# Pairwise sums of the weight blocks: moving those of the down projection from the second attention into the first gate-and-up stage

## The chip, the cores and the metric

One Trainium2 chip; the kernel uses one of its cores. The metric is device time in microseconds (us) of one launch. Lower is better.

## The reference, cut to what matters

One layer (DEPTH = 1): a chunked attention with a relative-position bias, then a SwiGLU feed-forward network (FFN), each between two RMS norms. 2048 tokens, width 1024, 16 heads of 64, d_ff 2816, all in float32.

```python
h = rms_norm(x, g_pre_mix)
m = chunk_relpos_attention(h, w_qkv, w_o, rel_bias)   # chunk c of 64 sees chunks c-8..c
x = x + rms_norm(m, g_post_mix)
h = rms_norm(x, g_pre_ffn)
x = x + rms_norm((silu(h @ w_gate) * (h @ w_up)) @ w_down, g_post_ffn)
```

## The kernel before, in words

**Precision.** Each float32 operand is split into a rounded part `hi` and a rest `lo`; a product is three TensorE (PE) matmuls (`products`, lines 189 to 191). The text calls these three a *triple*.

**Stages.** The tokens form two groups of 1024 (`NG` = 2), each with two halves of 512. In order of time: attention of group 0, attention of group 1 (their query, key, value and output products interleaved with scores, softmax and values), then for each group `gate_up(g, ...)` and `down(g, ...)`. The attentions are driven by a loop over 64 slots per group at the end of the code; in each slot `Attend.scores` and `Attend.transposed` run with dense products as fill.

**Seven products instead of eight.** Gate, up and down are 2x2 block products done with seven block multiplications (a Strassen-Winograd scheme). Four of the seven need weight blocks that are sums of given blocks, called S1 to S4. These sums do not depend on the tokens. They are made once, in DRAM, by DMAs alone: `copy` writes one block to its place (SP's queue), and `add` adds another to it with an accumulating DMA (POOL's queue, line 857). A *unit* is one slice of the weights: 11 units for gate and up (blocks of 512 KB, tensors `gu_S`), 11 for down (256 KB, `d_S`), with four copies and four adds each. `weight_sums` is a generator of *steps*; the copies of unit u stand in steps 4u to 4u+3, its adds in steps 4u+5, 4u+6, 4u+8 and 4u+11. The copies are put on SP's queue behind the last DMA issued there, the adds on POOL's behind the last softmax scaling (`pool.tensor_scalar`, line 566).

**When the steps are issued before.** 22 units give 96 steps; slot m of the 128 slots of both attentions issues the next step whenever `m * 96 // 120` grows: 0.8 step per slot. Gate and up come first, so nearly all of their sums fall in the first attention, and those of down in the second.

**Order.** The order of PE is written out by hand. On each other engine the instructions run in one fixed order too. Side work (norms, late residual sums, loads for later) waits in the queue `later`; each triple of PE earns one unit of credit (`tick`), and a step of `later` runs when its cost is there.

**The first gate-and-up stage.** `gate_up(0, ...)` runs 11 rounds of seven products, each of 8 triples. Each product takes one 512 KB weight block, loaded up to four products ahead (`ffn_ahead`), split on ACT and DVE. Beside it, `later` holds: a pause, then for two halves `Late.sums`, `Late.rstd` and `Late.write`, then `Blocks.sums`. `Late.write` is, eight times for each half and ten credits apart: load `y` and `res` to two of three `io` buffers, normalise on DVE (line 1136), add on DVE (line 1139), store. `Late.rstd` sends its sums through PE, DVE, POOL (a power, line 259) and PE again (`prs`, line 271). All plain DMAs are issued by SP, in order (line 68).

**Gathers.** At the end of an attention `gather` loads the heads' outputs (`al<-attn`) and ACT and DVE split them (lines 341 and 342).

Of the kernel before, what the change touches and what calls it, by code (L numbers as in the profile page):

```python
# [47 lines left out]
def trunk(  # L48
# [158 lines left out]
    def drain():  # L207
        while later:
            later.popleft()[1]()
# [15 lines left out]
    def narrow(name):  # L225
        return scratch(name)[:, :HALF]
# [610 lines left out]
    NC = NF // 2  # L837

    def gate_up_at(c):
        return {n: w_gu[c, BLOCK_AT[n]] for n in BLOCK_AT}, {n: sum_gu[n][:, c, :] for n in sum_gu}  # L840

    def down_at(c):
        return {n: w_d[BLOCK_AT[n]][:, c, :] for n in BLOCK_AT}, {n: sum_d[n][:, c, :] for n in sum_d}

    units = [gate_up_at(c) for c in range(NC)] + [down_at(c) for c in range(NC)]

    def weight_sums():

        def copy(to, a):
            with tc.issue_after(last_sp[0].ins):
                sp.dma_start(to, a)

        def add(to, a):
            with tc.issue_after(last_pool[0].ins):
                pool.dma_start(to, a, accum_op=ALU.add)

        steps = [[] for _ in range(4 * len(units) + 8)]
        for u, (src, dst) in enumerate(units):  # L860
            for n, (to, a) in enumerate((("S1", "A21"), ("S3", "A11"), ("S2", "A11"), ("S4", "A12"))):
                steps[4 * u + n].append((copy, dst[to], src[a]))
            for n, to, a in ((5, "S1", src["A22"]), (6, "S3", src["A21"]), (8, "S2", dst["S1"]), (11, "S4", dst["S2"])):
                steps[4 * u + n].append((add, dst[to], a))
        for step in steps:
            yield [f(to, a) for f, to, a in step]
# [11 lines left out]
    def ffn_take():  # L878
        ffn_ahead(used[0])
        used[0] += 1  # L880
        return made[used[0] - 1]
# [39 lines left out]
    def bank(name):  # L921
        return phase["psf"].tile([P, HALF], F32, tag="pd", name=name, bufs=6)

    def gate_up(g, b):


        big = xp.tile([P, 10, HALF], F32, tag="big", name="terms", bufs=1)

        def product(pts, name, first, after):
            hi, lo = ffn_take()  # L930
            for i in range(2):
                for k in range(4):
                    c = slice(i * HALF + k * P, i * HALF + k * P + P)
                    products(
                        pts[i], hi[:, c], lo[:, c], b.t[name][:, 0, k, :], b.t[name][:, 1, k, :],
                        first and k == 0, k == 3, not first,
                    )
                    yield 3 * C512
                after(i)

        def finish(gate, up):

            dve.tensor_tensor(gate, gate, up, op=ALU.mult)

        for c in range(NC):
            p1, p5, u2 = ([big[:, 3 * n + c % 2, :], big[:, 3 * n + 2, :]] for n in range(3))
            t = {}

            def copy(pts, dst):
                return lambda i: act.activation(dst[i], pts[i], AF.Copy)  # L950

            def put(n):
                sp.dma_start(a_d[g][n][:, c, :], t[n])

            def c11(i):
                if i == 0:
                    t["B11"] = narrow("b11")
                    act.activation(t["B11"], pa[0], AF.Silu)
                else:
                    finish(t["B11"], pa[1])  # L960
                    put("B11")

            def u(i):
                dve.tensor_tensor(u2[i], p1[i], pb[i], op=ALU.subtract)
                dve.tensor_tensor(p5[i], p5[i], p1[i], op=ALU.add)

            def closing(pts, terms, then, op=ALU.subtract):
                def go(i):
                    dve.tensor_tensor(terms[i], pts[i], terms[i], op=op)  # L969
                    if i == 0:  # L970
                        act.activation(terms[0], terms[0], AF.Silu)
                    else:
                        finish(*terms)
                        then(terms[0])

                return go

            def sum_(n, a, b_, to=None, op=ALU.subtract):
                t[n] = narrow(n) if to is None else to
                dve.tensor_tensor(t[n], a, b_, op=op)  # L980

            def c12(x_):
                t["B12"] = x_
                sum_("T1", t["B11"], x_)
                put("T1")

            def c22(x_):
                t["B22"] = x_
                put("B22")
                sum_("T3", t["B12"], x_, t["B12"])  # L990
                put("T3")
                sum_("T2", x_, t["T1"], op=ALU.add)
                put("T2")

            def c21(x_):
                t["B21"] = x_
                put("B21")
                sum_("T4", x_, t["T2"])
                put("T4")

            pa = [bank("pa") for _ in range(2)]
            yield from product(pa, "B11", True, copy(pa, p1))
            yield from product(pa, "B21", False, c11)
            pc = [bank("pc") for _ in range(2)]
            yield from product(pc, "T1", True, copy(pc, p5))
            pb = [bank("pb") for _ in range(2)]
            yield from product(pb, "T2", True, u)
            yield from product(pc, "B22", False, closing(pc, u2, c12, ALU.add))
            yield from product(pb, "T3", False, closing(pb, p5, c22))
            yield from product(pb, "T4", False, closing(pb, p1, c21))  # L1010
# [243 lines left out]
    def dense():  # L1254
# [59 lines left out]
        for g in range(NG):  # L1314
# [9 lines left out]
                    later.extend(late.sums(6.0) + late.rstd(6.0) + late.write(10.0))  # L1324
            yield from gate_up(g, blocks[g])
            drain()
            if g == 0:
                halves = [Late(y_d[t], POST_FFN, x1_d[i + t], out[i + t]) for t in range(2)]
                later.extend(blocks[1].all(12.0))

                def spill(t, dt, here, put):
                    dst = narrow("y")
                    put(dst)
                    sp.dma_start(y_d[t][:, dt, :], dst)

                yield from down(g, spill)
                drain()
                continue
# [58 lines left out]
    phase["ap"] = stack_a.enter_context(tc.tile_pool(name="ap", bufs=2))  # L1397
    phase["psa"] = stack_a.enter_context(tc.tile_pool(name="psa", bufs=2, space=PSUM))

    sums = weight_sums()  # L1400
    n_sums = 4 * len(units) + 8
    work = dense()
    spent = [0.0]
    owed = [0.0]
# [21 lines left out]
    for g in range(NG):  # L1426
        until(("start", g))
        spent[0] = owed[0] = 0.0
        jobs = [Attend(g, i % 2, i // 2) for i in range(2 * NPAIR)]

        due, total = [], 0.0
        for p in range(NPAIR):
            if p == 0:
                seq = [("qk", 1), ("v", 1)] if g > 0 else []
            else:
                seq = [("qk", 0), ("qk", 1)] + ([("v", 0), ("v", 1)] if p % 2 == 0 else [])
            for kind, s in seq:
                total += QK_COST if kind == "qk" else V_COST
                i = 2 * p + s
                due.append((4 * i - 2.4 if kind == "qk" else 4 * i + 4, total))  # L1440
        slots = 8 * NPAIR
        for t in range(-1, slots):
            left = [(c - spent[0]) / max(d - t, 0.5) for d, c in due if c > spent[0]]
            rate = max(left + [3.0 if t < slots - 6 else 3.9])
            if t + 1 < slots:
                job = jobs[(t + 1) // 4]
                until(("qk", g, job.s, job.p))
                job.scores((t + 1) % 4)
                m = slots * g + t
                if m > 4 and (m * n_sums) // 120 > ((m - 1) * n_sums) // 120:  # L1450
                    next(sums, None)
            fill(0.25 * rate)
            if t > 0 and t % 4 == 0:
                i = t // 4 - 1
                jobs[i].output()

                fill(0.2 * rate if i < 2 * NPAIR - 2 else 0.0)
            else:
                fill(0.2 * rate)
            if t >= 0:  # L1460
                jobs[t // 4].transposed(t % 4, lambda: fill(0.45 * rate))
            fill(0.1 * rate)
            for s in range(2):
                if (g, s) not in ats and ("qk", g, s, NPAIR - 1) in said and ("pv", g, s, NPAIR - 2) in said:
                    gather(g, s)
        fill(2.0)
        jobs[-1].output()
    for _ in sums:
        pass
    for c in work:  # L1470
        tick(c / (3 * C512))
# [60 lines left out]
```

## Time and profile before

| what | value |
|---|---|
| median of 3 runs | 2447.63 us (2445.1 to 2448.66) |
| profiled execution | 2441.23 us, span 2439.5 us |
| mean granted PE clock | 0.995 |
| PE busy | 2400.2 us, 98% |
| DVE, ACT, POOL busy | 1466.2, 1033.1, 299.2 us |
| DMA moved | 488.41 MB, mean 200 GB/s |
| attention of group 0 and 1 | to about 500 us, and to about 1090 us |
| gate and up of group 0 | first matmul at 1149.4 us |
| down of group 0 | first matmul at 1577.6 us |

The profile is of one execution. A busy share is an average over stages. The share called DMA is the mean busy share of the core's 16 DMA engines; SP's DMAs appear as queue q1, POOL's as q0. The clock column gives the share of full speed that PE was granted.

### The profile page before, as it was taken

How to read it: one execution, taken by the hardware profiler on the slowest of the kernel's cores; microseconds unless marked ns; L12 is line 12 of the kernel's file. 1: busy time of each engine (PE TensorE's matmuls, PEld its weight loads, DVE VectorE, ACT ScalarE, POOL GpSimd, SP SyncE). 2: the span in 40 equal slices, each digit the busy share in tenths (PEclk: the TensorE clock that was granted, in tenths of full speed). 3: DMA queues.
4: the chain of work that ended last, by engine and by line, in shares of the span. 5: the costliest groups of instructions: out<-in, count | busy, mean ns of one | idle time of the engine just before them, and what ended most of it. 6: DMA issues, size and time to landing. Idle time of an engine off the chain costs nothing.

```text
span 2439.5 us, 34920 instructions
## 1 busy us (share of the span) xinstructions
PE 2400.2 (98%) x12554; PEld 1994.3 (82%) x12554; DVE 1466.2 (60%) x2569; ACT 1033.1 (42%) x1807; POOL 299.2 (12%) x379
## 2 busy tenths in 40 slices
PE   9999999899999999999999999999999999999997
PEld 8887887688888888778888788888888888888886
DVE  6555454577455554567567665577566655555577
ACT  5444444554344443455333333365343333334444
POOL 0223333202232322310000000000000000000001
PEclk9999999999999999999999999999999999999999
DMA  7689999957777766646476755477667655457654
GB/s 223 179 213 245 257 263 230 271 185 211 197 192 189 181 157 144 163 146 229 152 260 206 244 174 167 123 247 256 208 211 250 219 178 160 136 169 243 196 187 147
DMA packets 209884, 488.41 MB, mean 200 GB/s; under 512 B 25360, under 2 KB 27424, under 8 KB 208432
## 3 DMA queue, kind: packets, MB, share of 16 engines
q1 hardware_dynamic: 197040, 451.59, 58.4%
q0 software_dynamic: 12672, 34.61, 9.2%
q8 instruction: 99, 1.62, 0.3%
q14 instruction: 73, 0.60, 0.1%
HBM read 356.54 MB, written 148.42 MB: 207 GB/s over the span
## 4 chain that ended last, share of the span: by engine, by line
PE 52%; DMA 2%; DVE 2%; issue 0%; ACT 0%; SPq 0%; DVEq 0%; ACTq 0%
PE pd L190 6%; PE pd L189 6%; PE pd L191 6%; PE pb L189 4%; PE pb L191 4%; PE pb L190 4%; PE pa L189 3%; PE pa L191 3%; PE pa L190 3%; PE pc L189 3%; PE pc L190 3%; PE pc L191 3%; PE mm L189 1%; PE mm L191 1%; PE mm L190 1%; DMA y<-y 1%
## 5 line engine op out<-in xcount | busy, mean ns | idle before, releaser
L562 ACT ACTIVATE sc<-sc,nmax 128x640 f32<-128x640 f32 (+4 forms) x256 | 193.3, 756 | 280.7 <-DVE nmax L558 279.8
L189 PE MATMUL mm<-hb,whi 128*128 128x512 f32 x704 | 290.7, 413 | 3.5 <-ACT y L236 3.5
L191 PE MATMUL mm<-hb,wlo 128*128 128x512 f32 x704 | 277.6, 394 | 0.0
L190 PE MATMUL mm<-hb,whi 128*128 128x512 f32 x704 | 276.5, 393 | 0.0
L566 POOL TENSOR_SCALAR sc<-sc,rows 128x640 f32<-128x640 f32 (+4 forms) x256 | 194.1, 783 | 512.1 <-DVE rows L565 498.8
L558 DVE CUSTOM_DVE_ANT_0 sc<-st,bias 128x640 f32<-128x640 f32 (+4 forms) x256 | 179.8, 738 | 103.5 <-PE st L550 100.8
L189 PE MATMUL pb<-hb,whi_gu_T 128*128 128x512 f32 x528 | 206.1, 390 | 3.5 <-DVE terms L969 3.5
L190 PE MATMUL pb<-hb,whi_gu_T 128*128 128x512 f32 x528 | 205.5, 389 | 0.0
L191 PE MATMUL pb<-hb,wlo_gu_T 128*128 128x512 f32 x528 | 205.4, 389 | 0.0
L259 POOL TENSOR_TENSOR rs<-ms,neg_half 128x4 f32<-128x4 f32 (+1 forms) x11 | 16.7, 1520 | 1246.8 <-DVE ms L257 1246.8
L189 PEld LDWEIGHTS mm<-hb,whi 128*128 128x128 f32 x704 | 133.1, 189 | 38.1 <-issue 14.7
L191 PEld LDWEIGHTS mm<-hb,wlo 128*128 128x128 f32 x704 | 132.7, 188 | 29.3
L190 PEld LDWEIGHTS mm<-hb,whi 128*128 128x128 f32 x704 | 133.5, 190 | 19.5
L190 PE MATMUL pd<-a,whi_d_T 128*128 128x512 f32 (+1 forms) x368 | 140.0, 380 | 0.4 <-DVE a L342 0.4
L189 PE MATMUL pd<-a,whi_d_T 128*128 128x512 f32 (+1 forms) x368 | 140.0, 381 | 0.0
L191 PE MATMUL pd<-a,wlo_d_T 128*128 128x512 f32 (+1 forms) x368 | 139.7, 380 | 0.0
L189 PE MATMUL pa<-hb,whi_gu_B 128*128 128x512 f32 x352 | 137.5, 391 | 0.5 <-ACT terms L950 0.5
L549 PE MATMUL st<-k,q 128*128 128x384 f32 (+1 forms) x448 | 132.7, 316 | 4.9 <-DVE nmax L558 3.0
L191 PE MATMUL pa<-hb,wlo_gu_B 128*128 128x512 f32 x352 | 137.0, 389 | 0.0
L190 PE MATMUL pa<-hb,whi_gu_B 128*128 128x512 f32 x352 | 137.0, 389 | 0.0
L189 PE MATMUL mm<-whi,hb 128*128 128x256 f32 x448 | 132.8, 296 | 0.0
L126 DVE TENSOR_TENSOR wlo_gu_T<-raw,whi_gu_T 128x1024 fp32r<-128x1024 f32 x88 | 107.5, 1221 | 42.1 <-ACT whi_gu_T L125 41.7
(219 smaller groups left out, 5640.3 us busy)
## 6 DMA issues: line engine op xcount, KB each, us to landing
raw<-gu_S SPq DMA_DIRECT2D x88, 512.0 KB, 3.9
raw<-in_w_gu SPq DMA_DIRECT2D x66, 512.0 KB, 4.0
q<-stage SPq DMA_DIRECT2D x128, 256.0 KB, 5.4
y<-y SPq DMA_DIRECT2D x96, 256.0 KB, 3.9
gu_S<-in_w_gu SPq DMA_DIRECT2D x44, 512.0 KB, 6.9
raw_a<-aT SPq DMA_DIRECT2D x88, 256.0 KB, 3.6
raw_d<-d_S SPq DMA_DIRECT2D x88, 256.0 KB, 3.5
raw<-in_w_a SPq DMA_DIRECT2D x42, 512.0 KB, 5.4
```

The costliest lines, as they stand in the source:

```text
L126: dve.tensor_tensor(lo, raw, hi.bitcast(F32), op=ALU.subtract)
L189: pe.matmul(pt, a_hi, b_hi, start=first, stop=False, skip_group_check=go_on)
L190: pe.matmul(pt, a_hi, b_lo, start=False, stop=False, skip_group_check=go_on)
L191: pe.matmul(pt, a_lo, b_hi, start=False, stop=last, skip_group_check=go_on)
L259: pool.tensor_tensor(r[0][:, :nb], m[:, :nb], neg_half.to_broadcast([P, nb]), op=ALU.pow)
L549: pe.matmul(st[:, a:b], q[:, 2 * h, cols], kk[:, h, key], start=True, stop=False)
L558: dve.tensor_tensor_reduce(out=sc[:, :n], in0=st[:, c0 : c0 + n], in1=rev, scale=-1.0, scalar=3.0e38, op0=ALU.add, op1=ALU.min, accum_out= ...
L562: act.activation(sc[:, :n], sc[:, :n], AF.Exp, bias=nmax, scale=-1.0, accum_out=rows[:, 0:1])
L566: last_pool[0] = pool.tensor_scalar(sc[:, :n], sc[:, :n], rows[:, 1:2], 1.0, op0=ALU.mult, op1=ALU.mult)
```

## The change

The one generator of 22 units becomes two of 11. The steps for gate and up alone (52 of them) are spread over the slots of both attentions: 0.43 step per slot instead of 0.8. The steps for down (52 as well) leave the attentions: one is issued after each product of `gate_up(0, ...)`, until they are used up in the 52nd of its 77 products. A loop after `gate_up` would issue what is left. The copies and adds themselves, their sizes and their number stay.

```diff
-    units = [gate_up_at(c) for c in range(NC)] + [down_at(c) for c in range(NC)]
-
-    def weight_sums():
+    def weight_sums(units):
...
                     yield 3 * C512
                 after(i)
+            if g == 0:
+                next(sums_d, None)
...
             yield from gate_up(g, blocks[g])
             drain()
+            for _ in sums_d:
+                pass
...
-    sums = weight_sums()
-    n_sums = 4 * len(units) + 8
+    sums_gu, sums_d = (weight_sums([at(c) for c in range(NC)]) for at in (gate_up_at, down_at))
+    n_sums = 4 * NC + 8
...
                 if m > 4 and (m * n_sums) // 120 > ((m - 1) * n_sums) // 120:
-                    next(sums, None)
+                    next(sums_gu, None)
...
-    for _ in sums:
+    for _ in sums_gu:
         pass
```

The function whose steps are issued, unchanged but for its argument:

```python
def weight_sums(units):
    def copy(to, a):
        with tc.issue_after(last_sp[0].ins):
            sp.dma_start(to, a)

    def add(to, a):
        with tc.issue_after(last_pool[0].ins):
            pool.dma_start(to, a, accum_op=ALU.add)

    steps = [[] for _ in range(4 * len(units) + 8)]
    for u, (src, dst) in enumerate(units):
        for n, (to, a) in enumerate((("S1", "A21"), ("S3", "A11"), ("S2", "A11"), ("S4", "A12"))):
            steps[4 * u + n].append((copy, dst[to], src[a]))
        for n, to, a in ((5, "S1", src["A22"]), (6, "S3", src["A21"]), (8, "S2", dst["S1"]), (11, "S4", dst["S2"])):
            steps[4 * u + n].append((add, dst[to], a))
    for step in steps:
        yield [f(to, a) for f, to, a in step]
```

## The prediction, made before the changed kernel was run

> **What bounds the kernel now.** I read the page first, then a table of busy time by stage, then the waits of the one stage in which PE loses time, then the landing times of DMAs in several stages, and last the chain of waits in the stage that the sums are moved to.
>
> ```profile
> span 2439.5 us, 34920 instructions
> PE 2400.2 (98%) x12554; PEld 1994.3 (82%) x12554; DVE 1466.2 (60%) x2569; ACT 1033.1 (42%) x1807; POOL 299.2 (12%) x379
> ```
>
> PE is the bound, with 39 us of its span idle. Nothing in this change touches a matmul, so it can only act through time in which PE stands still or is granted a lower clock. The table by stage says where that is (columns: stretch in us, length, then busy time of each engine, granted clock, DMA share, GB/s).
>
> ```profile
> 200.00:350.00 150.00, 149.97 (x931) 123.81 (x930) 80.24 (x212) 62.16 (x144) 45.31 (x64) 1.00 0.96 262
> 350.00:500.00 150.00, 136.69 (x817) 111.36 (x816) 78.53 (x185) 68.37 (x146) 38.69 (x53) 0.97 0.94 251
> 640.00:790.00 150.00, 149.71 (x964) 124.16 (x963) 82.82 (x188) 65.59 (x129) 43.47 (x54) 1.00 0.76 197
> 1000.00:1100.00 100.00, 95.87 (x530) 75.56 (x529) 63.86 (x130) 49.56 (x91) 20.29 (x25) 0.98 0.58 165
> 1140.00:1225.00 85.00, 85.00 (x381) 70.52 (x380) 53.54 (x70) 38.95 (x54) 1.42 (x1) 1.00 0.56 180
> 1225.00:1275.00 50.00, 49.04 (x219) 40.29 (x218) 35.21 (x47) 16.62 (x22) 0.00 (x0) 1.00 0.78 250
> 1275.00:1420.00 145.00, 142.84 (x637) 118.09 (x636) 92.54 (x123) 53.04 (x72) 1.93 (x1) 1.00 0.68 218
> 1420.00:1560.00 140.00, 140.00 (x631) 116.24 (x630) 80.54 (x105) 50.84 (x68) 2.01 (x2) 1.00 0.51 161
> ```
>
> Three things are to be seen. The end of the first attention (350 to 500) loses 13.3 us of PE and has a clock of 0.97, worth 0.03 x 150 = 4.5 us more: 17.8 us. The end of the second (1000 to 1100) loses 4.1 us and 0.02 x 100 = 2.0 us: 6.1 us, at a DMA share of 0.58 instead of 0.94. The first gate-and-up stage (1140 to 1560) loses 3.1 us, and its DMA share lies between 0.51 and 0.78. A high DMA share alone is harmless: from 200 to 350 it is 0.96 and PE loses nothing. It hurts where an engine stands in its queue for a landing. At the end of the first attention that is so (waits, and the rows of the gathered tile, first the one then the other attention):
>
> ```profile
> PE mm L189 <- ACT y L236: 3.5, 1, 3.5
> PE po L611 <- ACT pT L587: 3.4, 1, 3.4
> PE st L549 <- DMA k<-stage: 1.8, 2, 1.7
> ACT hb L341 <- DMA al<-attn: 15.2, 9, 3.5
> ...
> DMA to landing us min/median/max: 3.3/6.0/10.6
> ...
> DMA al<-attn: 7.8, 6
> ...
> DMA to landing us min/median/max: 2.5/3.5/6.0
> ```
>
> ACT waits 15.2 us for gathered tiles that land after 6.0 us, and PE then waits for ACT; in the second attention the same tiles land after 3.5 us and ACT waits 7.8 us.
>
> **The change, part by part.** Nothing is removed. 44 copies and 44 adds of 256 KB go from the second attention to the first gate-and-up stage, and those of 512 KB are thinned from 0.8 to 0.43 step per slot (54%) and reach into the second attention.
>
> *First attention.* What the sums take of the DMA engines there (queues and issues from 350 to 420):
>
> ```profile
> q1 hardware_dynamic: 4137, 11.03, 47.9%
> q0 software_dynamic: 1296, 4.72, 44.0%
> ...
> gu_S<-in_w_gu SPq DMA_DIRECT2D x6, 512.0 KB, 8.3
> ```
>
> The adds hold 44.0%. A copy holds about 0.479 x 70 us / 11.03 MB x 0.524 MB = 1.6 us, six of them in 70 us 14%. Thinning takes away 46% of that 58%, 27 points, so the share falls from 0.94 to about 0.67. Between the two ends of attention, 0.94 with 17.8 us lost and 0.58 with 6.1 us, a straight line gives a gain of 11.7 x 27/36 = 8.8 us. I take 8. Ends: 0, since the waits named on PE are for ACT and DVE too and may be those of the hand-written order; and 17.8 if all of it goes.
>
> *Second attention.* Bytes per slot go from 0.8 x 256 KB to 0.43 x 512 KB, 8% up. PE lost 0.3 us from 640 to 790 at a share of 0.76. I take 0, between -1 and +2 (a single wait for keys like the 1.8 us above).
>
> *Gate and up, DMA demand.* The price of a 256 KB sum is read where they ran, 700 to 900:
>
> ```profile
> q1 hardware_dynamic: 13202, 29.97, 51.1%
> q0 software_dynamic: 3024, 5.51, 19.5%
> ...
> q<-stage SPq DMA_DIRECT2D x28, 256.0 KB, 5.6
> ...
> raw<-in_w_a SPq DMA_DIRECT2D x8, 512.0 KB, 4.7
> ```
>
> An add holds the 16 engines 0.195 x 200 / 5.51 x 0.262 = 1.86 us, a copy by q1's mean 0.511 x 200 / 29.97 x 0.262 = 0.89 us. A unit of four and four: 11.0 us. The steps come one per product. The pace of PE is in the chain:
>
> ```profile
> 1227.82 0.23 PE pa L189
> ...
> 1231.23 0.23 PE pa L189
> ```
>
> Five triples in 3.41 us, so 0.68 us a triple, 5.46 us a product; a unit is issued each 21.8 us and adds 0.50 to the DMA share, from 1149 for 52 x 5.46 = 284 us, to 1433. On top of the table: 1.06, then 1.28 (1225 to 1275), then 1.18. More than there is, for most of the stage. What is late next is what waits for a landing in an engine's queue: the late residual sums. Their chain:
>
> ```profile
> 1240.56 0.70 DVE y L1139
> ...
> 1241.28 0.32 SPq L68
> ...
> 1241.69 4.93 DMA res<-in_x
> ...
> 1246.72 0.70 DVE y L1139
> ...
> 1262.07 0.75 DVE y L1136
> 1262.82 0.61 DVE terms L969
> 1263.47 0.50 PE pb L189
> ```
>
> The add on DVE frees a buffer, SP issues the next load, and DVE stands in its queue until that lands: one turn is 6.16 us (1240.56 to 1246.72), of which 4.93 us is the landing. PE allows ten credits a turn, 6.8 us. So the landing may grow by 0.65 us, from 4.9 to about 5.6, before the loop is slower than PE. Beyond that DVE falls behind; behind its wait stand the evacuations of PE's banks, and the last three rows show PE waiting for them already now. How much do landings grow? The nearest rows are those of 200 to 350, at a share of 0.96:
>
> ```profile
> q<-stage SPq DMA_DIRECT2D x24, 256.0 KB, 7.2
> ...
> raw<-in_w_a SPq DMA_DIRECT2D x8, 512.0 KB, 6.4
> ```
>
> They are 1.6 and 1.7 us above those of 700 to 900. With +1.6 a turn is 7.75 us, 0.95 over the pace, and all 16 turns lie beside the sums:
>
> ```profile
> L1139 DVE TENSOR_TENSOR y<-res,y x16: 678/693/695, 1231.2 to 1368.8; 128x512 f32<-128x512 f32 x16
> ```
>
> 16 x 0.95 = 15 us. Ends: 0, if landings stay under 5.6 us; and the demand over capacity itself, 0.06 x 76 + 0.28 x 50 + 0.18 x 145, and nothing after 1420, = 45 us, if PE is held to the pace of the DMA engines and no add falls behind. A gain of more than the 3.1 us that PE loses there now is excluded.
>
> *Weight loads* of 512 KB would go from 4.7 to 6.4 us by those rows; they are issued four products (21.8 us) before use, and only their split on ACT, one product (5.46 us) after the issue, can stand in its queue, by 1 us. ACT is busy 46% there. I take 0; if ACT's cover is gone, up to 1 us for each of 52 products is within the 45 us above.
>
> *SP's queue.* 44 issues move with the copies; at the 0.32 us of the issue in the chain above they take 14 us of SP in 284 us, and a copy waits for nothing. 0.
>
> *POOL's queue.* The adds now stand ahead of the power of `Late.rstd`, for which PE's `prs` transposes wait.
>
> ```profile
> 1222.09 1.42 POOL L259 TENSOR_TENSOR rs<-ms,neg_half 128x4 f32<-128x4 f32 x1 [147.92 <-DVE ms L257]
> ...
> POOL gu_S L857 <- issue: 112.8, 30, 7.3
> ...
> POOL d_S L857 <- issue: 10.5, 7, 2.7
> ...
> 1226.69 0.44 PE prs L271 x4
> ```
>
> The power ends at 1223.5 and is needed at 1226.7: 3.2 us of cover. A small add stalls POOL for 2.7 us at most and takes 0.85 us itself: 3.6, so 0.4 us late; with 7.3 us, as at the large adds, 5 us. Two such places: 0 to 10 us, I take 1.
>
> Sum: -8 + 0 + 15 + 1 = +8 us on the profiled execution's 2441.2: 2449.2. The median of the runs stands 6.4 us above that execution, so 2455.6 for the median, say 2456.
>
> [...] With both queues loaded, from 350 to 420, POOL's queue held 44.0% and SP's 47.9%. [...]
>
> The clock fell to 0.97 where PE had waits of 3.4 and 3.5 us, and not in 1225 to 1275 where it lost 1 us. [...]
>
> **The rivals.** *Faster:* the landing of `res` stays under 5.6 us, because POOL waits before its adds (112.8 us in 30 places) spread them by themselves past 1433, where the share is 0.51 and no one needs the down sums before 1577. Then only the first attention counts: -8, a median of 2440. For it: 0.96 from 200 to 350 without loss. Against it: there DVE had no load to wait for, and q0 took its 0.44 regardless. It decides at a mean landing of 5.6 us.
>
> *The DMA engines become the bound* of the stage: all 45 us less some 10 for adds that drain later, and -8: +27, 2475; the whole 45 gives 2485. For it: a demand of 1.18 to 1.28. Against it: POOL's waits thin out that demand.
>
> *No change to be seen:* the loop loses about what the attention gains, or the gain is nil as the order by hand sets it and the landings hold: 2443 to 2452.
>
> **How the numbers follow.** A measurement of this kernel can tell about 0.2%, 4.9 us, from no change. Chances: forecast 0.45 (2453 to 2467), faster 0.26 (2434 to 2442), DMA-bound 0.13 (2467 to 2490), no change 0.16. So faster 0.26, same 0.16, slower 0.58. The range 2435 to 2483 leaves out the best of the faster case and the worst of the DMA-bound one.
>
> **What would show it.** Right: DMA share from 350 to 500 near 0.7, `al` landing near 4 us, PE idle there under 8 us; share from 1150 to 1430 at 0.95 or more; `res` landing at 6.5 us; waits of DVE line 1139 and 1136 for DMA several times today's, and of PE `pb` for DVE line 969 in many places. Wrong: `res` landing under 5.6 us, or PE idle at the end of the first attention as before with a share of 0.7, or stalls of `prs` for POOL of several us.

## The result

The changed kernel takes 2471.92 us (median; 2470.22 to 2477.97) where the kernel before takes 2446.6 on the same chip: a ratio of 1.0104, 95% interval 1.0085 to 1.0123. It is slower, by 25 us. Its profiled execution took 2470.22 us, 29.0 us more than that of before. Of the executions timed below, one of experiment 1 (5860.55 us) and one of experiment 5 (5480.89 us), more than twice as long as all others, are left out of the medians.

The page, and the table by stage, of the changed kernel:

```profile
span 2468.4 us, 34893 instructions
PE 2404.1 (97%) x12554; PEld 1996.4 (81%) x12554; DVE 1463.8 (59%) x2569; ACT 1031.6 (42%) x1807; POOL 298.2 (12%) x379
```

```profile
350.00:500.00 150.00, 141.50 (x850) 114.84 (x849) 81.94 (x192) 71.52 (x151) 31.78 (x44) 0.98 0.77 215
640.00:790.00 150.00, 148.41 (x954) 122.65 (x953) 83.09 (x188) 66.07 (x130) 37.60 (x47) 1.00 0.76 196
1000.00:1100.00 100.00, 95.52 (x526) 75.49 (x523) 67.57 (x133) 51.99 (x96) 17.58 (x21) 0.98 0.54 167
1140.00:1225.00 85.00, 85.00 (x383) 70.52 (x382) 52.91 (x70) 36.82 (x51) 11.40 (x13) 1.00 0.90 251
1225.00:1275.00 50.00, 44.43 (x185) 36.21 (x184) 28.21 (x39) 13.41 (x17) 6.63 (x8) 0.93 0.97 294
1275.00:1420.00 145.00, 119.79 (x519) 98.21 (x518) 77.55 (x103) 41.73 (x56) 16.89 (x21) 0.92 0.86 253
1420.00:1560.00 140.00, 140.00 (x631) 116.24 (x630) 81.36 (x107) 51.29 (x69) 6.14 (x7) 1.00 0.62 192
```

From 350 to 500 PE is idle for 8.5 us instead of 13.3. From 1225 to 1420 it is idle for 30.8 us instead of 3.1. The cleanest account takes no busy times at all, only the moments at which two stages start. First the kernel before, then the changed one:

```profile
L189 PE MATMUL pa<-hb,whi_gu_B x144: 389/389/484, 1149.4 to 1473.0; 128*128 128x512 f32 x144
...
L189 PE MATMUL pd<-a,whi_d_B x132: 389/389/389, 1577.6 to 1696.6; 128*128 128x512 f32 x132
```

```profile
L189 PE MATMUL pa<-hb,whi_gu_B x143: 389/389/496, 1143.5 to 1499.9; 128*128 128x512 f32 x143
...
L189 PE MATMUL pd<-a,whi_d_B x95: 389/389/389, 1605.6 to 1699.5; 128*128 128x512 f32 x95
```

The first gate-and-up stage starts 5.9 us earlier, lasts 462.1 us instead of 428.2, and the rest to the end of the span takes 862.8 instead of 861.9: -5.9 + 33.9 + 0.9 = 28.9 us. So the question is what the 33.9 us are. From the first matmul of this stage to the first of down, PE stands still for 30.8 us instead of 3.1, and is busy for 431.3 us instead of 425.1 with the same matmuls: 27.7 us of waiting and 6.2 us of slower matmuls. The waits of PE name two things, here in the changed kernel and then before:

```profile
PE prs L271 <- POOL rs L259: 22.1, 2, 20.6
PE pb L189 <- DVE terms L969: 11.0, 3, 5.6
```

```profile
PE pb L189 <- DVE terms L969: 3.5, 3, 2.2
...
PE prs L271 <- POOL rs L259: 1.5, 1, 1.5
```

The 20.6 us are one single wait, for the power of the second late half. Here is DVE's input to that power, and then POOL's list at that time:

```profile
1318.53 0.16 DVE L257 TENSOR_SCALAR ms<-pssq 128x4 f32<-128x4 f32 x1 [0.79 <-PE pssq L255]
```

```profile
1316.46 0.84 POOL L855 DMA_DIRECT2D d_S<-in_w_d  x1 [6.73 <-issue]
1323.32 0.82 POOL L855 DMA_DIRECT2D d_S<-in_w_d  x1 [6.02 <-DMA res<-in_x]
1327.79 0.84 POOL L855 DMA_DIRECT2D d_S<-d_S  x1 [3.64 <-issue]
1333.15 0.82 POOL L855 DMA_DIRECT2D d_S<-d_S  x1 [4.52 <-issue]
1337.50 0.83 POOL L855 DMA_DIRECT2D d_S<-d_S  x1 [3.53 <-issue]
1342.03 0.82 POOL L855 DMA_DIRECT2D d_S<-d_S  x1 [3.69 <-DMA d_S<-d_S]
1342.58 1.33 POOL L259 TENSOR_TENSOR rs<-ms,neg_half 128x4 f32<-128x4 f32 x1
```

The power's input is there at 1318.7; the power starts at 1342.6, because after that moment five more adds stand ahead of it, one every 4.3 to 7 us. An add keeps POOL itself for 0.8 us; the rest, in brackets, is POOL waiting before it can issue the next. Over the 19 adds from 1227 to 1342 one starts 6.4 us after the other on average.

### The profile page after: what moved, and what is told of

The parts are those of the page before. It is cut to its first block, busy times and chain, and to the rows that moved or that the text cites. A ratio compares the mean times of both kernels' runs of the same rounds, so it can differ in the third digit from the quotient of the medians.

```text
span 2468.4 us, 34893 instructions
## 1 busy us (share of the span) xinstructions
PE 2404.1 (97%) x12554; PEld 1996.4 (81%) x12554; DVE 1463.8 (59%) x2569; ACT 1031.6 (42%) x1807; POOL 298.2 (12%) x379
## 5 line engine op out<-in xcount | busy, mean ns | idle before, releaser
L190 PEld LDWEIGHTS mm<-hb,whi 128*128 128x128 f32 x704 | 133.1, 189 | 19.4
L259 POOL TENSOR_TENSOR rs<-ms,neg_half 128x4 f32<-128x4 f32 (+1 forms) x11 | 16.1, 1466 | 1014.8 <-DVE ms L257 1014.8
```

Of the source, the lines that this page charges most:

```text
L190: pe.matmul(pt, a_hi, b_lo, start=False, stop=False, skip_group_check=go_on)
L259: pool.tensor_tensor(r[0][:, :nb], m[:, :nb], neg_half.to_broadcast([P, nb]), op=ALU.pow)
```

## The experiments

All times in the table are from the profiled executions: when the first gate-and-up stage starts, how long it lasts to the first matmul of down, and PE's waits (for the powers, including 1.5 us at the start of the kernel; for DVE at `pb`, all lines together). The medians and ratios are over the timed executions, the ratios against the kernel before on the same chip (medians of 2446.0 to 2446.7 us).

| kernel | stage starts | lasts | for powers | for DVE | median | ratio (95%) |
|---|---|---|---|---|---|---|
| before | 1149.4 | 428.2 | 1.5 | 3.5 | 2446.6 | 1 |
| changed | 1143.5 | 462.1 | 22.1 | 11.0 | 2471.9 | 1.0104 (1.0085 to 1.0123) |
| 1 power on ACT | 1143.8 | 440.7 | 1.5 | 11.8 | 2451.5 | 1.0019 (1.0004 to 1.0034) |
| 2 two of three products | 1141.9 | 456.1 | 14.2 | 12.1 | 2463.6 | 1.0072 (1.0057 to 1.0087) |
| 3 gate and up early | 1146.4 | 468.5 | 23.3 | 14.5 | 2480.4 | 1.0144 (1.0122 to 1.0167) |
| 4 more DMA scratch memory | 1141.5 | 458.3 | 11.4 | 15.6 | 2466.3 | 1.0083 (1.0068 to 1.0098) |
| 5 power on ACT and pause | 1142.3 | 433.2 | 1.5 | 6.1 | 2439.9 | 0.9969 (0.9952 to 0.9986) |
| 6 pause alone | 1142.9 | 461.8 | 25.4 | 5.0 | 2468.5 | 1.0088 (1.0056 to 1.0121) |
| 7 before, power on ACT | 1149.8 | 427.3 | 1.5 | 1.8 | 2446.3 | 1.0001 (0.9981 to 1.0022) |
| 8 no down adds | 1145.5 | 430.1 | 1.5 | 4.3 | 2438.8 | 0.9967 (0.9950 to 0.9985) |
| 9 power first | 1140.8 | 451.7 | 4.6 | 18.6 | 2455.8 | 1.0031 (1.0012 to 1.0051) |
| 10 power first and pause | 1147.2 | 443.5 | 1.5 | 13.1 | 2453.3 | 1.0024 (1.0007 to 1.0040) |

Stage starts and lengths are of one execution each. The nine kernels that spread the gate and up sums as the changed one does start this stage between 1140.8 and 1147.2 us, so a difference of a few us in these columns alone says little.

**1. The power on ACT.** In `rstd_steps`, while `gate_up(0)` runs:

```diff
-            pool.tensor_tensor(r[0][:, :nb], m[:, :nb], neg_half.to_broadcast([P, nb]), op=ALU.pow)
+            if beside[0]:
+                act.activation(r[0][:, :nb], m[:, :nb], AF.Abs_reciprocal_sqrt)
+                return
+            pool.tensor_tensor(r[0][:, :nb], m[:, :nb], neg_half.to_broadcast([P, nb]), op=ALU.pow)
```

> The changed kernel, but in the first gate-and-up stage alone the power of the norm is an inverse square root on ACT instead of a power on POOL. Theory A (queue): PE's 22.1 us of waits for line 259 come from a backlog of accumulating DMAs on POOL, which takes about 6.2 us for each while the steps come every 5.46 us; the power stands behind it. Then the wait goes, and the time falls by 20 to 26 us from 2472, to 2446 to 2452. Theory B (DMA engines): the 25 us are the price of a DMA demand above what there is; then the time taken out there comes back at other waits, and it falls by less than 8 us, to 2464 or more.

```profile
PE pb L190 <- DVE terms L973: 11.8, 4, 6.6
...
PE prs L275 <- POOL rs L263: 1.5, 1, 1.5
```

The wait is gone (the 1.5 us are at the start of the kernel), the stage is 21.4 us shorter and the median falls by 20.4 us, inside the 20 to 26 of theory A. The adds, the copies and their rate are untouched, and nothing came back elsewhere. Theory B has fallen.

**2. A step after two of three products.**

```diff
-            if g == 0:
+            turns[0] += 1
+            if g == 0 and turns[0] % 3:
                 next(sums_d, None)
```

> The changed kernel, but a step of the down sums follows only two of three products, so all 52 are spread over 77 products. Theory A: an add comes every 8.2 us on average, POOL needs about 6.2, no backlog builds up; PE's wait for line 259 falls from 22.1 us to under 5 us, and the time by 18 to 28 us, to 2444 to 2454. Theory B: demand falls by a third, to 0.9 to 1.1 of what there is, so the time falls as well, by 10 to 18 us, but PE's wait for line 259 stays above 10 us, as adds are then slow for want of DMA engines and not of a place in POOL's queue.

```profile
PE prs L271 <- POOL rs L259: 12.5, 2, 11.0
PE pb L189 <- DVE terms L971: 12.1, 4, 6.6
```

Neither came out whole: 8.3 us less time, where A gave 18 to 28 and B 10 to 18, and a wait of 12.5 us (1.7 more for another power, `hr`) that A had under 5 and B above 10. With a step every 8.2 us and the 6.4 us that an add took in the changed kernel, no backlog should form. So theory A named the queue rightly, but not why the adds stand ahead of the power. That is taken up in 4, 6 and 9.

**3. The gate and up sums at 0.8 step per slot, as before.**

```diff
-    n_sums = 4 * NC + 8
+    n_sums = 8 * NC + 8
```

> The changed kernel, but the gate and up sums are issued at 0.8 step per slot as in the kernel before, so nearly all fall in the first attention; the down sums stay in the gate-and-up stage. If the spreading is what gained at the end of the first attention, PE idle and lost clock from 350 to 500 go back from 11 to about 18 us, and the time is 5 to 9 us above the changed kernel, 2477 to 2481. If that part was luck of the order, the time stays within 3 us of 2472. PE's wait for line 259 stays at about 22 us in both.

```profile
350.00:500.00 150.00, 137.73 (x814) 111.19 (x813) 78.03 (x185) 67.58 (x146) 39.00 (x53) 0.95 0.90 240
...
1000.00:1100.00 100.00, 97.81 (x550) 77.69 (x549) 67.22 (x135) 51.02 (x94) 16.29 (x20) 1.00 0.51 160
```

From 350 to 500 PE idles 12.3 us at a clock of 0.95 again, against 8.5 us at 0.98 in the changed kernel: the gain there is due to the thinner sums. But from 1000 to 1100, where this kernel has no sums left, it loses 2.2 us where the changed one loses 4.5. By the start of the stage the spreading is worth only 1146.4 - 1143.5 = 2.9 us, which is inside the spread of starts given under the table. The median moved by 8.5 us, as expected, but 6.4 us of that profile's difference lie in the gate-and-up stage (468.5 against 462.1), which this edit was not meant to touch. How the net gain of the attentions divides between thinner sums and fewer sums is not settled more finely than that.

**4. Four times the DMA scratch memory.**

```diff
-    nc = bacc.Bacc("TRN2", target_bir_lowering=False, num_devices=1, dynamic_dma_scratch_size=512)
+    nc = bacc.Bacc("TRN2", target_bir_lowering=False, num_devices=1, dynamic_dma_scratch_size=2048)
...
-        rows[1] = const.tile([P, HALF], F32, name="rstd_1")
+        rows[1] = rows[0]
```

> The changed kernel with four times the memory for POOL's DMA descriptors (2048 instead of 512 bytes a partition). To make room, the first group's second half shares the first half's row of norms, so this kernel's values differ; its instructions are otherwise the same. If POOL's 6.2 us per add is the wait for room for descriptors (A'), POOL issues an add in about 1 us, the backlog and PE's wait for line 259 go, and the time falls by 18 to 26 us. If an add is slow for another reason (B'), POOL keeps its 6 us per add and the time stays within 6 us of 2472; if more adds in flight crowd the loads, PE's waits for DVE line 969 grow above 11 us.

POOL's waits before its adds, first in the changed kernel, then here:

```profile
POOL d_S L855 <- issue: 107.5, 21, 7.3
```

```profile
POOL d_S L855 <- issue: 0.9, 2, 0.6
```

So the waits before adds that name nothing else in the profile go with this setting: at 512 they are 107.5 us, at 2048 0.9 us. That POOL waits there for room for descriptors is the author's reading; no run shows what the memory holds. Yet the wait for the powers only halved:

```profile
PE pb L189 <- DVE terms L969: 13.4, 3, 6.9
PE prs L271 <- POOL rs L259: 11.4, 2, 9.9
```

The median fell by 5.6 us, between A' and B'. The power still stands behind adds, and POOL's waits before these are now for an earlier copy or add to land: for `d_S<-in_w_d` 282.8 us in 32 waits, instead of 149.5 in 11 in the changed kernel. The last case of the expectation came as well: PE's waits for DVE grew from 11.0 to 15.6 us (2.2 of them at line 964).

**5 and 6. A pause in the steps**, from the norm of a late half to the end of its writes; in 5 the power is on ACT as well, in 6 it is on POOL.

```diff
-            if g == 0:
+            if g == 0 and not hold[0]:
                 next(sums_d, None)
...
-                    later.extend(late.sums(6.0) + late.rstd(6.0) + late.write(10.0))
+                    later.extend(late.sums(6.0) + holding(True) + late.rstd(6.0) + late.write(10.0) + holding(False))
```

> The changed kernel with the power on ACT in the first gate-and-up stage, as in the run with a median of 2452, and with no step of the down sums issued from the norm of a late half to the end of its eight writes (22 of 77 products are skipped, 55 stay for the 52 steps). Theory C: what is left of the loss, 11.8 us of PE's waits for DVE and a clock of 0.93, comes from the sums' DMAs delaying the loads and stores of those writes. Then these waits fall to 4 us or less, as in the kernel before, and the time is 8 to 13 us under that run, 2438 to 2444, below the kernel before. Rival D: the stage is short of DMA time wherever the steps stand; then other waits take their place and the time stays at 2449 to 2454.

```profile
PE pb L190 <- DVE terms L978: 6.1, 3, 2.7
```

```profile
1225.00:1275.00 50.00, 47.31 (x202) 38.67 (x201) 30.11 (x40) 14.02 (x18) 0.00 (x0) 0.97 0.78 251
1275.00:1420.00 145.00, 142.76 (x629) 117.83 (x628) 93.89 (x125) 55.45 (x75) 10.77 (x13) 0.99 0.84 258
```

Theory C holds, with DVE's part at 6.1 us rather than 4. From 1225 to 1275, where the first half is written, the DMA share is 0.78 as before the change; PE idles 4.9 us from 1225 to 1420 instead of 30.8, and the time, 2439.9 us, is under that of the kernel before (2446.0 on that chip). All the sums are still made in this stage.

> The same pause in the steps, but the power stays on POOL. If the power is late because of the backlog of adds issued before it, these are still ahead of it: PE's wait for line 259 is 5 to 15 us, the time 2447 to 2459. If it is late only because POOL's fixed order puts it behind adds whose copies come later in the program, the pause takes those away, the wait falls under 2 us, and the time is that of the kernel with the power on ACT and the same pause, 2438 to 2444.

```profile
PE prs L276 <- POOL hr L264: 19.4, 1, 19.4
PE prs L276 <- POOL rs L264: 6.0, 2, 4.5
```

The wait at the second power fell from 20.6 to 4.5 us, and a new one of 19.4 us appeared at the third, of the next group's norm: the adds that the pause pushed back stand in front of it. The sum, 25.4 us, is no smaller, and the time, 2468.5 us, was in neither range.

**7. Control: the kernel before with the power on ACT.**

> Control: the kernel before, with the power on ACT in the first gate-and-up stage. There no add stands on POOL at that time and PE did not wait for it, so nothing is to be gained: within 3 us of 2446.6. If loading ACT's tables costs something on the path, up to 5 us more.

2446.3 us, a ratio of 1.0001. The move to ACT is worth nothing by itself; it helps only where adds stand on POOL.

**8. No adds of the down sums.**

```diff
-            for n, to, a in ((5, "S1", src["A22"]), (6, "S3", src["A21"]), (8, "S2", dst["S1"]), (11, "S4", dst["S2"])):
+            for n, to, a in () if units is down_units else ((5, "S1", src["A22"]), (6, "S3", src["A21"]), (8, "S2", dst["S1"]), (11, "S4", dst["S2"])):
```

> The changed kernel without the 44 adds of the down sums (the copies stay, so the down weights are not summed); the power is on POOL. Theory A: nothing stands ahead of the power, PE's wait for line 259 is under 2 us. For PE's waits for DVE, 11 us in the changed kernel: if the adds' share of the DMA engines, two thirds of what the sums need, delays the loads of the writes, the waits fall under 5 us and the time is 2436 to 2443; if it is the copies in SP's own queue, they stay at 8 to 13 us and the time is 2446 to 2452.

```profile
PE pb L189 <- DVE terms L969: 4.3, 3, 2.0
```

Both costs go, the second one too: with the copies alone on SP's queue, PE's waits for DVE are 4.3 us. So SP's 44 issues are not what costs. The adds are, but this run does not tell how: without them the DMA share from 1225 to 1275 is 0.84 instead of 0.97, and their place on POOL is empty too.

**9 and 10. The power ahead of later adds**, without and with the pause. `add` issues behind `last_pool`; the power now counts as such:

```diff
-            pool.tensor_tensor(r[0][:, :nb], m[:, :nb], neg_half.to_broadcast([P, nb]), op=ALU.pow)
+            last_pool[0] = pool.tensor_tensor(r[0][:, :nb], m[:, :nb], neg_half.to_broadcast([P, nb]), op=ALU.pow)
```

> The changed kernel, but the adds that the program issues after a power are put behind that power in POOL's list (the power counts as POOL's last instruction for them). Only POOL's list differs: the second power stands eight adds further ahead. Theory E (order): in the changed kernel the list, fixed before the run, has the power behind adds that the program issues after it; the backlog is long because of these. Then PE's wait for line 259 falls from 22.1 us to under 3 us, and the time to that with the power on ACT, 2447 to 2453. Theory A as first put (adds issued before the power, at 6.2 us each against 5.46 us a step, are what it waits for): these are still ahead of it, the wait stays above 8 us, and the time at 2458 or more.

```profile
PE pb L189 <- DVE terms L969: 16.5, 3, 8.1
PE prs L271 <- POOL rs L259: 4.6, 2, 3.1
```

Only POOL's list differs from that of the changed kernel, the lists of the four other engines are the same. Moving the second power ahead of seven adds (31 start before it in the changed kernel, 24 here; the expectation said eight) takes its wait from 20.6 to 3.1 us or less. Theory E holds for most of the wait: the power stood behind adds that the program issues *after* it, since `add` asks only to come behind the last softmax scaling. The adds issued earlier hold it up by some 3 us. But the time fell by 16.1 us only, not by the 19 to 25 of theory E, while the waits for DVE grew from 11.0 to 18.6 us (another 2.1 at line 964).

> The same order on POOL and the pause of the steps from the norm of a late half to the end of its writes; the power stays on POOL. By theory E both costs of the moved sums are gone: PE's waits for line 259 under 3 us (three powers, the third of them that of the next group's norm, which the pause pushed adds in front of), those for DVE 4 to 6 us, and a time of 2437 to 2443, as with the power on ACT and the pause. If the adds issued before the third power still hold it up, that wait stays above 8 us and the time at 2448 or more.

```profile
PE pb L189 <- DVE terms L974: 8.3, 2, 4.7
...
PE pb L189 <- DVE terms L969: 4.8, 3, 2.0
```

In the stage the powers are no longer waited for, but DVE is, by 13.1 us instead of the 4 to 6 expected, and the 2453.3 us miss the range. Five adds that now stand behind the first power run from 1222 to 1249, in the middle of the writes that the pause was to keep free. That these adds are the cause was read from the order on POOL, not tried by itself.

## Why the prediction was right, and where it was not

The direction and the range held: 2471.9 us in 2435 to 2483, slower. The likeliest case, 2456 with its own 2453 to 2467, did not: the loss was 29 us of profiled time and not 8. The parts as measured are -5.9 (attentions), +12.5 (late writes), +21.4 (POOL's queue) and +0.9 (the rest). That the range held is luck: its upper part was there for a rival whose cause did not come, and the largest part of the loss lies outside the ends given for its term.

*What bounds the kernel:* right. PE's work is the same, and the stage's 33.9 us are PE standing still (27.7) or slowed (6.2).

*First attention, -8.* The mechanism was right (`al` lands sooner, ACT waits less), its size was a little too high:

```profile
DMA al<-attn: 11.3, 5
...
DMA to landing us min/median/max: 2.6/5.3/8.0
```

The landing fell from 6.0 to 5.3 us, not to near 4, and the DMA share to 0.77, not 0.67. Idle time and lost clock went from 17.8 to 8.5 + 3.0 = 11.5 us: -6.3. Over both attentions -5.9 was left at the start of the next stage.

*Second attention, 0:* 1.6 us idle from 640 to 790 instead of 0.3, inside the range given.

*The late writes, +15.* With the power out of the way (experiment 1) the stage is 440.7 - 428.2 = 12.5 us longer, so the term had about the right size. Its working held in part: it had the landing of `res` grow by 1.6 us and all 16 turns late by 0.95 us. The landing, before and then changed:

```profile
DMA to landing us min/median/max: 3.0/4.9/5.9
...
DMA to landing us min/median/max: 2.9/5.2/8.3
```

At the median it grew from 4.9 to 5.2 us and stayed under the 5.6 at which the loop was to fall behind. But the longest grew from 5.9 to 8.3 us, and DVE's wait for `res` from 3.7 to 12.7 us (21.8 us in experiment 1). The loads of `y`, which the term left out, grew more: of those issued from 1225 to 1420, some of them for the next half's norm, the median went from 4.0 to 6.2 us. PE pays in two single waits, 5.6 and 4.6 us; the third of the row, 0.8 us, is in the second group. The second runs along the other way through the buffers, a store and then the load that takes its place, in the chain of waits of the changed kernel:

```profile
1389.71 5.30 DMA x<-y
...
1395.04 4.31 DMA y<-y
...
1399.43 0.06 DVE y L1136
...
1404.65 0.61 DVE terms L969
...
1405.31 0.80 PE pb L189
1406.10 0.43 PE pb L190
...
1408.95 0.23 PE pb L191
```

DVE stands for 9.6 us of store and load, works off what has gathered behind, and PE gets its bank at 1405.3. The prediction showed the end of such a chain but priced the `res` loop. That the DMAs of the sums make this cost is shown by experiments 5 and 8 (6.1 and 4.3 us of waits for DVE, instead of 11.0); that the way through the buffers is this one is read from one chain. After the wait a matmul takes 0.43 us, then 0.23 again; the granted clock from 1405 to 1410 is 0.66. The sum has no term for the clock, and 6.2 us of the stage are slower matmuls. The prediction set the clock of 0.97 at the end of the first attention beside waits of 3.4 and 3.5 us. These runs do not show that a wait must be so long. In experiments 5 and 6, where PE idles 2.7 and 2.8 us from 1225 to 1275, the clock there is 0.97; in the kernel before it is 0.74 from 420 to 430, after two waits of 1.5 and 1.7 us. And after its wait of 3.4 us, which ends at 457.5, the clock is 1.00 up to 462. So in these runs the clock was low after some waits under 3.4 us, and not low after one of 3.4 us.

*POOL's queue, +1, from 0 to 10.* This is the step that failed. It measured 21.4 us of stage (462.1 - 440.7), twice its upper end. Counting one add ahead of the power, at 2.7 + 0.85 us, was wrong twice: with its waits an add takes POOL 6.4 us in this stage (1227 to 1342, at a DMA share of 0.92), and the list had seven adds ahead of the power that come after it in the program (experiment 9).

*SP's queue and the weight loads, 0 each:* held. With the 44 copies alone (experiment 8) the stage lasts 430.1 us, 1.9 more than before, and no wait of PE in the changed kernel's stage names a weight block.

*The rivals.* "The DMA engines become the bound" gave 2475 us, near the measured time, and is wrong as a cause: at the same demand, experiment 1 takes 2451.5 us and experiment 5, which adds only a pause, 2439.9. "Faster" was held to depend on the landing of `res`; at the median that stayed under its mark, and still the kernel was slower, mostly for another reason.

*What would show it.* Of the signs of being wrong, two came: `res` landing under 5.6 us, and, as the last item, "stalls of `prs` for POOL of several us". Of the signs of being right, DVE's wait for `res` came; `res` did not land at 6.5 us, and PE waited for DVE line 969 in two places, not in many.

## What to carry to other kernels

Before work is moved onto an engine's queue that looks idle, list what else stands in that queue and how soon someone needs it: one small instruction, on a path to the bottleneck, behind DMAs that take POOL some 6 us each cost 21.4 us of this stage, against 12.5 us for all else there. Price an accumulating DMA on its issuing engine by the distance between two such issues in a busy stage (here 6.4 us), not by its own 0.85 us, and look at the fixed order of the list, as an instruction may stand behind work that the program issues later. Where a stage has its own short chain of loads and stores, spread background DMAs around that chain, not evenly: with that and the power on another engine, the same sums in the same stage gave 2439.9 us against 2446.0 for the kernel before on that chip.

## What the runs showed that I had not expected

One setting ends most of POOL's waits before adds that name nothing else: with `dynamic_dma_scratch_size` at 512 they are 107.5 us, at 2048 0.9 us. And the sums did not slow all loads of this stage alike: from 1225 to 1420 the median landing of `y` (256 KB) went from 4.0 to 6.2 us and that of the weight blocks `in_w_gu` (512 KB) from 4.2 to 6.9, while `res` (256 KB) went only from 4.9 to 5.2 over its 16 loads, with 8.3 us for the longest instead of 5.9.
